# Moving the buffers of streamed operands off their common 2048-byte phase in SBUF

## The chip, the cores and the metric

The kernel runs on one core of a Trainium2 chip. The metric is the device time of one execution in microseconds; where several runs are shown, the median counts. A core has TensorE (PE: matmuls, and loads of the block of weights that stays resident in the array), VectorE (DVE), ScalarE (ACT), GpSimd (POOL) and SyncE (SP, which issues the DMAs here). Operands lie in SBUF, 128 partitions side by side; an address below is a byte offset within each partition. Results of matmuls go to PSUM.

## The reference

Two layers over 1024 tokens of width 1024, in float32. Layer 0 mixes tokens by attention over a sliding window of 128, with a sink and partial rotary embedding; layer 1 by a gated linear recurrence (HGRN2). Each is followed by an MLP of width 4096.

```python
for layer in range(DEPTH):
    h = rmsnorm(x, mix_norm[layer])
    y = sliding_window_attention(h, ...) if layer % 2 == 0 else hgrn2_recurrence(h, ...)
    x = x + y
    h = rmsnorm(x, mlp_norm[layer])
    x = x + jnp.square(jax.nn.relu(h @ w_up[layer])) @ w_down[layer]
return rmsnorm(x, final_norm)
```

## The kernel before, in words

**Tiles.** Everything large is cut into tiles of 128 partitions by 512 floats (TH), which is 2048 bytes in each partition. The tokens are handled in two halves (NH) of 512. Each tile belongs to a tag, and BUFS (line 41) says how many buffers a tag has: 60 of "a", 18 of "t", 7 of "m", 5 each of "wr", "wh" and "wl". "p" and "q" are four PSUM tiles each. "a" holds what lives long: the residual stream x, the operands that PE streams against many weight blocks, sums of the down projection. "t" holds what lives briefly, "wr" raw weights as they come from memory, "m" sums of weights and the scores of the attention.

**A product.** A float32 product is made of three passes in a faster format: split (line 429) and weight_split (line 412) cut a value into a high part, which is a cast, and a low part, which is the difference to it. mm3 (line 394) then multiplies high by high, high weights by low operand, low weights by high operand, all into one PSUM tile. In the large products the resident block is 128 columns of "wh" or "wl" and the streamed operand is an "a" tile, whole (512 columns) or half (256); in the projection of the attention (qkv, line 1069) it is the other way round, with a block of "a" resident and the weights streamed. The rows of the profile name the streamed operand first: "p<-a,wh" streams "a" against a block of "wh". The products of the MLPs and of the recurrence's input are arranged by Strassen's scheme, so weights are added and subtracted on DVE ("m<-wr,wr") before they are split.

**The recurrence** (line 1353) forms its scores in six levels. In level lg each chunk of 64 columns is cut into blocks of H = 2^lg, and PE streams every second block (line 1361), which begins H floats into the chunk.

**Order.** Each operation is put down with its engine, cost, inputs and outputs, and a planner (order, line 185) plays the program through with these costs. It decides the order on every engine, which of two engines does a cast, and the slot of every buffer: when a buffer's last user is done, its slot goes back on a heap, and the next buffer of that tag takes the slot that came free first. The planner knows slots by their number, not by their address.

**Addresses.** issue (line 275) calls lay_out (line 473) before it emits the instructions. lay_out reserves SBUF in the order in which it asks: first eight small constants (lines 475 and 476), then each buffer of a, t, wr, wh and wl as one tile of 2048 bytes (lines 477 to 479). The small tiles ahead of them add up so that the first of these buffers begins on a multiple of 2048, and since each is 2048 bytes long, all 93 do. Tags that lay_out does not name (m, and constants made later) lie behind. An "m" buffer is as long as its largest tile, 128 by 4 by 130 floats, 2080 bytes. When an operation is emitted, View.place (line 76) asks Buf.handle (line 111) for the tile of its buffer, which takes the slot's place by the tag "a_17" and the like, and applies the slices of the view to it. All instructions are recorded under line 336.

**DMAs.** All go through SP's queue in the planner's order (dma, line 346): weights into wr, x into a and t, spilled tiles from a and t to memory ("d") and back, and at the end a to the output.

Of the kernel before, what the change touches and what calls it, by code (L numbers as in the profile page):

```python
# [2 lines left out]

# [7 lines left out]
F32 = mybir.dt.float32  # L11
# [6 lines left out]
P = 128  # L18
# [4 lines left out]
TH = T // NH  # L23
# [17 lines left out]
BUFS = {"a": 60, "t": 18, "m": 7, "sm": 8, "wr": 5, "wh": 5, "wl": 5, "p": 4, "q": 4}  # L41
CH = 64
LEVELS = 6
HOMES = "aaaaaaaaaaaa"
K_SPANS = ((-1, 3), (2, 6), (5, 8))


class View:
# [34 lines left out]
class Buf:  # L83
# [27 lines left out]
    def handle(self):  # L111
        if self.tile is None:
            tag = f"{self.tag}_{self.slot}"
            self.tile = self.pool.tile(self.shape, self.dtype, tag=tag, name=self.name, bufs=1)
        return self.tile


# [24 lines left out]
class Schedule:  # L142
# [132 lines left out]
    def issue(self, lay_out):  # L275
        ops = self.order()
        lay_out()
        for op in ops:
            op.ways[op.engine][0]()


class Net:
# [190 lines left out]
    def lay_out(self):  # L473

        for v in (self.par, self.ones, self.ident, self.prev_mask, self.mean, self.eps, self.neg, *self.square[:1]):
            v.buf.handle()
        for tag in ("a", "t", "wr", "wh", "wl"):
            for k in range(BUFS[tag]):
                self.pool.tile([P, TH], F32, tag=f"{tag}_{k}", name=f"{tag}_first{k}", bufs=1)

    def spread(self, y, n=TH, r=None):

# [553 lines left out]
    def k_tiles(self, i):  # L1036
        if self.ks[i] is None:
# [3 lines left out]
            for g, z in enumerate(self.kl[i]):  # L1041
                _, o = self.rows(g)
                self.memset(z[o].bitcast(F32).only("o"), 0.0, "Pool", late)
            if K_SPANS[i][0] < 0:
                for z in self.ks[i] + self.kl[i]:
# [51 lines left out]
    def keys_values(self, n, ps, r):  # L1097
# [14 lines left out]
        for gp in range(2):  # L1112
            self.transpose(pk[:, gp], k[:, gp * P : gp * P + P])
        for i, (first, end) in enumerate(K_SPANS):
            if not first <= n < end:
# [50 lines left out]
    def attend_block(self, g, n, stacks):  # L1166
        i = (n >= 3) + (n >= 6)
        c = slice((n - 1 - K_SPANS[i][0]) * P, (n + 1 - K_SPANS[i][0]) * P)
        tok = slice((n % BPH) * P, (n % BPH) * P + P)
# [485 lines left out]
```

## Time and profile before

| | us |
|---|---|
| median of 3 runs | 2102.72 |
| the three runs | 2101.64 to 2105.72 |
| the profiled execution | 2103.77 |
| its span, first to last instruction | 2102.0 |

A row of the costliest groups gives the line, engine and operation, output and inputs by tag, the shapes, the count, then busy microseconds and mean nanoseconds of one, then the idle time of the engine ahead of it and what ended that. "(+1 forms)" says that the group mixes shapes. A row of the timeline gives the start in microseconds from the span's start, the duration, and how many instructions were merged. A row of the chain gives start, duration and what held the chain. A row of waits gives who waited for whom, the sum, the number of times and the longest. A row of one tile gives minimum, median and maximum duration in nanoseconds. A row of the DMA issues gives the number, the size and the median time to landing.

### The profile page before, as it was taken

Reading aid. Unit: us, or ns where it says so; the run is one execution under the profiler, and the core shown is the slowest. Engines: PE = TensorE matmul, PEld = TensorE weight load, DVE = VectorE, ACT = ScalarE, POOL = GpSimd, SP = SyncE. Lnnn points to the kernel's source line nnn. Section 1 sums busy time; section 2 is a strip of 40 time slices with the busy share of each in tenths; the row PEclk is TensorE's granted clock in tenths of the full one; section 3 lists DMA queues with packets and bytes.
Section 4 is the critical chain, followed back from the end, with each engine's and each line's share of the span. In section 5 each row is a group of like instructions: output and inputs, shape, how many; then the busy total and the mean of one; then the engine's idle time right before and its main releaser. Section 6 shows DMA issues by size and latency. Waiting matters only on the chain.

```text
span 2102.0 us, 35648 instructions
## 1 busy us (share of the span) xinstructions
PE 2068.4 (98%) x12220; PEld 1738.6 (83%) x12220; DVE 1898.4 (90%) x3922; ACT 1120.0 (53%) x2284; POOL 61.0 (3%) x121
## 2 busy tenths in 40 slices
PE   9999999999999999999999999999999999999998
PEld 7778777888888887888888888888788888888887
DVE  8889899999999989999889888888999999998995
ACT  5567777656565323556444444443755656432453
POOL 4030000000000000000000000000000000000000
PEclk9999999999999999999999999999999999999999
DMA  6212277867778967732322232576787777896742
GB/s 214 79 51 81 86 239 245 297 224 248 231 240 289 313 220 245 236 136 76 101 98 99 96 101 97 202 234 221 270 267 229 244 228 250 284 321 211 238 133 80
DMA packets 225845, 407.43 MB, mean 194 GB/s; under 512 B 25344, under 2 KB 30464, under 8 KB 225664
## 3 DMA queue, kind: packets, MB, share of 16 engines
q1 hardware_dynamic: 225664, 405.16, 58.5%
q8 instruction: 96, 1.57, 0.3%
q14 instruction: 85, 0.70, 0.1%
HBM read 321.17 MB, written 83.89 MB: 193 GB/s over the span
## 4 chain that ended last, share of the span: by engine, by line
PE 38%; DVE 11%; DMA 4%; issue 3%; ACT 1%; POOL 0%; SPq 0%; POOLq 0%; DVEq 0%; ACTq 0%
PE p L336 22%; PE q L336 16%; DVE t L336 4%; DVE a L336 3%; DMA wr<-in_down 2%; DVE wl L336 2%; DVE m L336 2%; ACT t L336 1%; DMA t<-d 1%; DMA wr<-in_up 1%; DMA d<-t 0%; DVE wh L336 0%; DMA wr<-in_win 0%; DMA a<-d 0%; ACT wh L336 0%
## 5 line engine op out<-in xcount | busy, mean ns | idle before, releaser
L336 PE MATMUL p<-a,wh 128*128 128x512 f32 (+1 forms) x2880 | 809.9, 365 | 3.2 <-DVE a L336 2.4
L336 PE MATMUL q<-a,wh 128*128 128x512 f32 x2112 | 654.6, 391 | 7.4 <-ACT t L336 6.1
L336 PEld LDWEIGHTS p<-a,wh 128*128 128x128 f32 x2880 | 514.6, 189 | 89.1 <-DVE a L336 4.0
L336 PE MATMUL p<-a,wl 128*128 128x512 f32 (+1 forms) x1440 | 521.0, 362 | 0.4 <-DVE wl L336 0.4
L336 PEld LDWEIGHTS q<-a,wh 128*128 128x128 f32 x2112 | 389.1, 188 | 85.3 <-ACT t L336 8.4
L336 PE MATMUL q<-a,wl 128*128 128x512 f32 x1056 | 411.1, 390 | 1.7 <-DVE wl L336 1.7
L336 PEld LDWEIGHTS p<-a,wl 128*128 128x128 f32 x1440 | 271.6, 189 | 40.9 <-DVE wl L336 1.3
L336 DVE TENSOR_TENSOR wl<-wr,wh 128x512 fp32r<-128x512 f32 x352 | 240.8, 685 | 6.7 <-ACT wh L336 1.3
L336 DVE TENSOR_TENSOR wl<-m,wh 128x512 fp32r<-128x512 f32 x338 | 230.1, 686 | 10.6 <-ACT wh L336 1.4
L336 PEld LDWEIGHTS q<-a,wl 128*128 128x128 f32 x1056 | 198.3, 188 | 45.6 <-DVE wl L336 3.7
L336 ACT ACTIVATE t<-t 128x512 f32<-128x512 f32 x268 | 168.8, 632 | 122.3 <-DVE t L336 114.9
L336 ACT CAST wh<-wr 128x512 fp32r<-128x512 f32 x249 | 154.0, 619 | 142.8 <-PE p L336 94.7
L336 DVE TENSOR_TENSOR t<-t,t 128x512 f32<-128x512 f32 (+3 forms) x337 | 197.4, 599 | 17.0 <-DMA t<-d 9.9
L336 ACT CAST a<-t 128x512 fp32r<-128x512 f32 (+1 forms) x216 | 130.1, 611 | 148.5 <-PE q L336 78.7
L336 DVE TENSOR_TENSOR a<-t,a 128x512 fp32r<-128x512 f32 (+2 forms) x314 | 205.9, 677 | 2.2 <-ACT a L336 1.7
L336 ACT CAST wh<-m 128x512 fp32r<-128x512 f32 x231 | 143.1, 620 | 113.8 <-PE p L336 47.4
L336 ACT COPY t<-q 128x512 f32<-128x512 f32 (+2 forms) x201 | 112.2, 559 | 104.1 <-PE q L336 87.3
L336 DVE TENSOR_TENSOR m<-wr,wr 128x512 f32<-128x512 f32 (+1 forms) x188 | 120.9, 645 | 17.6 <-DMA wr<-in_down 13.0
L336 PE MATMUL p<-wh,a 128*128 128x512 f32 x384 | 124.9, 396 | 0.7 <-ACT a L336 0.7
L336 DVE TENSOR_TENSOR t<-t,p 128x256 f32<-128x256 f32 x294 | 118.0, 414 | 0.3
L336 PEld LDWEIGHTS q<-t,t 128*64 128x64 f32 (+1 forms) x2160 | 95.4, 144 | 13.6 <-issue 7.6
L336 PE MATMUL q<-t,t 128*64 128x32 f32 (+2 forms) x2160 | 105.3, 229 | 0.0
(129 smaller groups left out, 2392.7 us busy)
## 6 DMA issues: line engine op xcount, KB each, us to landing
t<-d SPq DMA_DIRECT2D x548, 256.0 KB, 4.1
d<-t SPq DMA_DIRECT2D x244, 256.0 KB, 2.7
wr<-in_down SPq DMA_DIRECT2D x224, 256.0 KB, 4.2
wr<-in_up SPq DMA_DIRECT2D x178, 256.0 KB, 3.9
wr<-in_win SPq DMA_DIRECT2D x68, 256.0 KB, 2.9
a<-d SPq DMA_DIRECT2D x60, 256.0 KB, 4.7
wr<-in_wqkv SPq DMA_DIRECT2D x48, 256.0 KB, 2.9
d<-a SPq DMA_DIRECT2D x48, 256.0 KB, 3.9
```

What stands on the lines that cost most here:

```text
L336: fn(*[place(a) for a in args], **{k: place(v) for k, v in kw.items()})
```

## The change

Every second buffer of "a", those with an odd number, is reserved 16 bytes (four floats) longer, and its data begins behind these 16 bytes. lay_out asks for the "a" buffers last, behind t, wr, wh and wl, so that those four tags still begin on multiples of 2048.

```diff
+SKIP = {f"a_{k}": 4 for k in range(1, BUFS["a"], 2)}
...
     def handle(self):
         if self.tile is None:
             tag = f"{self.tag}_{self.slot}"
-            self.tile = self.pool.tile(self.shape, self.dtype, tag=tag, name=self.name, bufs=1)
+            skip = SKIP.get(tag, 0)
+            if skip:
+                n = math.prod(self.shape[1:])
+                whole = self.pool.tile([self.shape[0], skip + n], self.dtype, tag=tag, name=self.name, bufs=1)
+                self.tile = whole[:, skip:]
+                if len(self.shape) == 3:
+                    self.tile = self.tile.rearrange("p (a b) -> p a b", a=self.shape[1])
+            else:
+                self.tile = self.pool.tile(self.shape, self.dtype, tag=tag, name=self.name, bufs=1)
         return self.tile
...
-        for tag in ("a", "t", "wr", "wh", "wl"):
+        for tag in ("t", "wr", "wh", "wl", "a"):
             for k in range(BUFS[tag]):
-                self.pool.tile([P, TH], F32, tag=f"{tag}_{k}", name=f"{tag}_first{k}", bufs=1)
+                name = f"{tag}_{k}"
+                self.pool.tile([P, TH + SKIP.get(name, 0)], F32, tag=name, name=f"{tag}_first{k}", bufs=1)
```

More of the change, by code (lines that the diff above doesn't have):

```diff
@@ L1 @@
 import heapq
+import math
 from contextlib import ExitStack
```

## The prediction

> **What bounds the kernel.** I read the page first: busy shares, granted clock, the costliest groups, the chain.
>
> ```profile
> span 2102.0 us, 35648 instructions
> ...
> PE 2068.4 (98%) x12220; PEld 1738.6 (83%) x12220; DVE 1898.4 (90%) x3922; ACT 1120.0 (53%) x2284; POOL 61.0 (3%) x121
> ...
> PEclk9999999999999999999999999999999999999999
> ...
> PE 38%; DVE 11%; DMA 4%; issue 3%; ACT 1%; POOL 0%; SPq 0%; POOLq 0%; DVEq 0%; ACTq 0%
> ...
> L336 PE MATMUL p<-a,wh 128*128 128x512 f32 (+1 forms) x2880 | 809.9, 365 | 3.2 <-DVE a L336 2.4
> L336 PE MATMUL q<-a,wh 128*128 128x512 f32 x2112 | 654.6, 391 | 7.4 <-ACT t L336 6.1
> ...
> L336 PE MATMUL p<-a,wl 128*128 128x512 f32 (+1 forms) x1440 | 521.0, 362 | 0.4 <-DVE wl L336 0.4
> ...
> L336 PE MATMUL q<-a,wl 128*128 128x512 f32 x1056 | 411.1, 390 | 1.7 <-DVE wl L336 1.7
> ```
>
> TensorE (PE) is busy for 98% of the span, its clock is full in every slice, and its four largest groups are the ones the change touches: in "p<-a,wh" the streamed operand is an "a" buffer, the resident weight block a "wh" buffer. Together these groups hold 2880 + 2112 + 1440 + 1056 = 7,488 matmuls. The chain covers only 57% of the span, but in what it covers PE has two thirds.
>
> Next, what PE waits for. The view of waits on PE has twelve rows; the first and the last are
>
> ```profile
> PE q L336 <- ACT t L336: 8.9, 11, 2.5
> ...
> PE p L336 <- DVE wl L336: 0.4, 1, 0.4
> ```
>
> and the twelve add up to 26.7 us, 1.3% of the span. So the kernel runs at the pace of PE's own stream, and the question is whether the address of a streamed operand sets that pace. Matmuls overlap, so their durations (365 to 391 ns) do not give the pace; the starts in the timeline do. A stretch with 512 columns and one with 256:
>
> ```profile
> 702.19 0.61 PE L336 MATMUL q<-a,wh 128*128 128x512 f32 x2
> 702.64 0.39 PE L336 MATMUL q<-a,wl 128*128 128x512 f32 x1
> ...
> 704.91 0.61 PE L336 MATMUL p<-a,wh 128*128 128x512 f32 x2
> ```
> ```profile
> 473.08 0.40 PE L336 MATMUL p<-a,wh 128*128 128x256 f32 x2
> 473.32 0.28 PE L336 MATMUL p<-a,wl 128*128 128x256 f32 x1
> ...
> 474.88 0.40 PE L336 MATMUL p<-t,wh 128*128 128x256 f32 x2
> ```
>
> Twelve matmuls start between 702.19 and 704.91: 2.72 / 12 = 226.7 ns each. Fifteen start between 473.08 and 474.88: 120.0 ns each. The 256 columns between the two sizes cost 106.7 ns, 0.417 ns a column; what is left, 120.0 - 106.7 = 13.3 ns, is a fixed gap of 32 column times in each matmul. That gap is the only part of the stream that could be a collision. Over the matmuls with an "a" buffer streamed (the 7,488, and 264 + 128 more of "p<-a,a" and "q<-a,a" below, 7,880 in all) it is 7,880 x 13.3 ns = 105 us.
>
> ```profile
> L336 PEld LDWEIGHTS p<-a,a x264: 187/192/192, 754.7 to 2090.5; 128*128 128x128 f32 x132
> ...
> L336 PEld LDWEIGHTS q<-a,a x128: 186/188/192, 82.8 to 276.0; 128*128 128x128 f32 x128
> ```
>
> **The change part by part.** No instruction is added, removed or reordered: the planner's costs and buffer numbers know nothing of addresses, and the tiles that lay_out reserves issue nothing. The five queues, SP's with its DMAs too, hold what they held. What changes is where things lie. The first tiles go t, wr, wh, wl, a, so the weights stay on multiples of 2048 bytes, and each odd "a" buffer leaves out 16 bytes ahead of its data. An "a" buffer then starts up to some hundred bytes past a multiple of 2048, so weights and streamed operand no longer begin at the same phase. What is allocated later (the m tiles, small constants) moves up. So the costs are those of reading and writing at other addresses, engine by engine.
>
> *PE, streamed operand.* No large matmul of before streams from such an address. The nearest rows are the small ones of the recurrence. Its levels stream columns that begin 2^level floats into their chunk: the second group of 64 instructions (levels 1 and 2) begins 8 and 16 bytes past the boundary, the third (levels 3 and 4) 32 and 64 bytes.
>
> ```profile
> 983.83 1.99 PE q L336 x64
> ...
> 993.29 1.99 PE q L336 x64
> ...
> 1003.67 1.99 PE q L336 x64
> ```
>
> Both take 1.99 us: a start of 16 bytes costs less than the 0.01 us the view resolves, under 0.2 ns an instruction. These matmuls have 32 columns and two share the array, so the row bounds without proving. For the range I let the long ones gain or lose four column times (the 16 bytes skipped are four columns): 7,880 x 4 x 0.417 ns = 13.1 us, either way; the whole gap, 105 us, is the far end below. I take 0, by the levels' rows and because the pace is the same 0.417 ns a column at both sizes.
>
> *PE, weight loads.* Where "a" is the resident block ("p<-wh,a"), a load at an odd address has a row: the transposes of the m tiles, whose rows are 130 floats, 520 bytes, apart, so that three in four start 8, 16 or 24 bytes past a multiple of 32.
>
> ```profile
> L336 PE MATMUL q<-c,t 128*128 128x128 f32 x136 | 22.0, 277 | 3.4 <-DVE t L336 1.9 <-ACT t L336 1.5
> ...
> L336 PE MATMUL q<-c,m 128*128 128x128 f32 x128 | 19.5, 275 | 0.5 <-DVE m L336 0.2
> ```
>
> 275 ns against 277 ns from aligned t: cost 0.
>
> *DVE and ACT.* The m tiles again give the row: 2080 bytes each, so they lie on no common multiple of 2048, while wr does.
>
> ```profile
> L336 DVE TENSOR_TENSOR wl<-wr,wh 128x512 fp32r<-128x512 f32 x352 | 240.8, 685 | 6.7 <-ACT wh L336 1.3 <-PE q L336 0.5 <-DVE wh L336 0.5
> L336 DVE TENSOR_TENSOR wl<-m,wh 128x512 fp32r<-128x512 f32 x338 | 230.1, 686 | 10.6 <-ACT wh L336 1.4
> ...
> L336 ACT CAST wh<-wr 128x512 fp32r<-128x512 f32 x249 | 154.0, 619 | 142.8 <-PE p L336 94.7 <-PE q L336 27.2 <-DMA wr<-in_down 5.5
> ...
> L336 ACT CAST wh<-m 128x512 fp32r<-128x512 f32 x231 | 143.1, 620 | 113.8 <-PE p L336 47.4 <-PE q L336 41.4 <-DVE m L336 24.8
> ...
> L336 DVE CAST wh<-m 128x512 fp32r<-128x512 f32 x107 | 45.6, 426 | 33.6 <-PE p L336 16.7 <-PE q L336 16.6
> ...
> L336 DVE CAST wh<-wr 128x512 fp32r<-128x512 f32 x103 | 43.5, 422 | 26.0 <-PE p L336 20.4 <-DMA wr<-in_wqkv 2.9 <-PE q L336 2.4
> ...
> L336 DVE CAST a<-t 128x512 fp32r<-128x512 f32 x18 | 7.6, 422 | 2.9 <-ACT t L336 1.6 <-DMA t<-d 1.2
> ```
>
> One to four ns either way; I take 0. The worst would be that a cast on DVE loses its quick form (422 against 685 ns): with "a" written there are 18 + 18 of them, with "a" read 24, so 60 x 263 ns = 15.8 us on an engine that is idle for 2102.0 - 1898.4 = 203.6 us. PE hides it; at DVE's 11% of the chain it would show as 1.7 us.
>
> *DMAs.* Rows of 2 KiB now begin inside a larger block.
>
> ```profile
> a<-d SPq DMA_DIRECT2D x60, 256.0 KB, 4.7
> ...
> d<-a SPq DMA_DIRECT2D x48, 256.0 KB, 3.9
> ...
> a<-in_x SPq DMA_DIRECT2D x16, 256.0 KB, 5.3
> ...
> out<-a SPq DMA_DIRECT2D x16, 256.0 KB, 2.1
> d<-a SPq DMA_DIRECT2D x24, 128.0 KB, 2.8
> ```
>
> No DMA of before shows such a start. From below the cost is nothing, since nothing is moved that was not. From above, a row that is cut in two costs what two half rows do: 2 x 2.8 - 3.9 = 1.7 us a transfer. Few are waited for. On the chain stands one into "a":
>
> ```profile
> 1942.21 4.94 DMA a<-d
> ```
>
> With four odd buffers among the first eight loads of x, and the last store, that is 1.7 x (1 + 4 + 1) = 10.2 us at most. I take 0: the row stays whole and 2 KiB long, nearest to the 3.9 us.
>
> [...]
>
> **The sum.** 0 on PE, DVE, ACT and DMA. The profiled execution took 2103.77 us, 1.8 us around its span of 2102.0; the median of the runs shown is 2102.72, 1.05 lower. So: 2103 us.
>
> **The rivals.**
>
> *A: faster, the gap was a collision.* Weights and streamed operand begin at the same phase in before; if the load of the next block (128 floats, 512 bytes, 32 pieces of 16 bytes) takes one column time from the stream for each piece, that would make exactly 32. For it: the number fits. Against it: weight blocks begin at 0, 512, 1024 and 1536 bytes, streamed halves at 0 or 1024, t and "a" alike, and the gap is 13.3 ns in both stretches; the loads of the two rows above last 186 to 192 ns throughout. Price: from -13 us (four column times: 2090) to -105 us (all: 1998). [...]
>
> *B: slower, a start inside a larger block costs a read more.* Place: every matmul that streams from "a"; price: four column times, +13 us, 2116; it decides from 4.2 us / 7,880 = 0.53 ns a matmul. For it: no long stream from such an address is in the trace, and PE has no slack. Against it: the 1.99 us of the levels.
>
> *C: slower by the DMAs.* +10 us, 2113, by the bound above; it needs the worst price at each place that waits.
>
> *The change does not do what it says*: if rounding of lengths put the buffers back on equal phases, the time would stay; this lies in the forecast.
>
> **How the numbers follow.** A measurement of this kernel can tell about 0.2%, 4.2 us, from no change (its three runs lie 4.1 us apart), so "same" is 2099 to 2107. No change has 0.49: every row at an odd address is level with its aligned twin, but none of them is a long stream. A has 0.22, of it 0.10 below 2088, since the 13.3 ns are there to be won in every matmul. B has 0.19, some 0.06 beyond 2120, where it costs more than four column times. C has 0.10. Faster is A; slower is B and C, 0.29. The range runs from A's near price with 2 us to spare, 2088, to B's with 4, 2120; outside lie 0.10 + 0.06 = 0.16.
>
> **What would show it.** Right: starts 226.7 and 120.0 ns apart as before, the four groups at 365, 391, 362 and 390 ns, wl<-m at 686 ns, "a<-d" landing in 4.7 us. A shows as a shorter pace at the same 0.417 ns a column; B as a longer one with only "a" streamed, while "p<-t,wh" stays at 120.0; C as longer landings of d<-a and a<-d with an unchanged pace, and longer waits of DVE for them. Wrong I am above all if a long stream behaves unlike one of 32 columns.

## The result, and the profile after

The changed kernel takes 2116.48 us (three runs, 2114.90 to 2118.24) against 2102.72: a ratio of 1.0062, 95% interval 1.0042 to 1.0081, so 13.8 us slower by the medians. The forecast of no change is wrong. The time lies inside the stated range of 2088 to 2120, where rival B had put it, but not for B's reason, as the experiments show.

The page of the changed kernel, the same parts as before:

```profile
span 2114.7 us, 35648 instructions
...
PE 2090.2 (99%) x12220; PEld 1737.4 (82%) x12220; DVE 1901.4 (90%) x3922; ACT 1121.6 (53%) x2284; POOL 60.6 (3%) x121
...
PEclk9999999999999999999999999999999999999999
...
L346 PE MATMUL q<-a,wh 128*128 128x512 f32 x2112 | 662.4, 395 | 2.5 <-ACT t L346 1.9
...
L346 PE MATMUL q<-a,wl 128*128 128x512 f32 x1056 | 415.4, 394 | 1.1 <-DVE wl L346 1.1
```

The instructions are the same in number, the clock is full as before (0.998 granted in both), DVE and ACT are busy for as long as before within 3 us. Only PE has more to do: 2090.2 us against 2068.4, and it now fills 99% of the span. A 512-column matmul lasts 4 ns longer (395 against 391, 394 against 390). That is inside the stream, not ahead of it: the idle time in front of the first group fell from 7.4 to 2.5 us.

The groups kept apart by shape show that the two sizes moved in opposite directions. After:

```profile
L346 PE MATMUL p<-a,wh 128*128 128x512 f32 x2096 | 672.2, 399 | 0.2 <-ACT t L346 0.2
...
L346 PE MATMUL p<-a,wh 128*128 128x256 f32 x784 | 143.8, 281 | 0.2 <-DVE t L346 0.2
...
L346 PE MATMUL p<-wh,a 128*128 128x512 f32 x384 | 126.1, 399 | 1.4 <-ACT a L346 1.4
```

and the same groups before:

```profile
L336 PE MATMUL p<-a,wh 128*128 128x512 f32 x2096 | 664.4, 395 | 2.9 <-DVE a L336 2.4 <-ACT t L336 0.5
...
L336 PE MATMUL p<-a,wh 128*128 128x256 f32 x784 | 145.5, 283 | 0.3 <-DVE t L336 0.3
...
L336 PE MATMUL p<-wh,a 128*128 128x512 f32 x384 | 124.9, 396 | 0.7 <-ACT a L336 0.7
```

512 columns: 395 to 399 ns. 256 columns: 283 to 281 ns, shorter. And "p<-wh,a", where the streamed operand is a weight buffer that still begins on a multiple of 2048 and only the resident block has another phase, went from 396 to 399 ns as well. A streamed read that costs a little more wherever it starts off its block fits neither of the last two.

The timeline of PE in the changed kernel gives the pace:

```profile
702.12 0.62 PE L346 MATMUL p<-a,wh 128*128 128x512 f32 x2
702.58 0.39 PE L346 MATMUL p<-a,wl 128*128 128x512 f32 x1
...
704.89 0.63 PE L346 MATMUL q<-a,wh 128*128 128x512 f32 x2
```

Twelve matmuls start between 702.12 and 704.89, 230.8 ns each; before it was 226.7. Over the whole trace, from the starts of all matmuls, leaving out distances over 245 ns (waits, and changes of kind): the 6,888 of 512 columns start 227.8 ns apart before and 231.9 after, 28.2 us more; the 1,764 of 256 columns with wh or wl 119.7 and 118.4 ns, 2.2 us less. What lies in those longer distances shrank by 13.4 us. The sum, about 12.6 us, is close to the growth of the span, 12.7 us (2114.7 - 2102.0). So a slower stream of 28 us shows as 13, because PE stood still for less time between its streams. One row of PE's waits shows where some of it went, after:

```profile
PE q L346 <- ACT t L346: 4.7, 9, 1.3
```

It was 8.9 us. All PE waits together are 17.6 us after and 26.7 before, so they name 9.1 of the 13.4 us; the rest lies in long distances that the view of waits does not name.

The even pace itself is gone: in before 5,249 of 6,674 such distances of 512 columns are 226 or 227 ns, in the changed kernel 472 of 6,682.

The other steps of the prediction, in the rows after:

```profile
a<-d SPq DMA_DIRECT2D x60, 256.0 KB, 4.4
...
d<-a SPq DMA_DIRECT2D x48, 256.0 KB, 3.9
...
a<-in_x SPq DMA_DIRECT2D x16, 256.0 KB, 5.4
...
out<-a SPq DMA_DIRECT2D x16, 256.0 KB, 2.2
...
d<-a SPq DMA_DIRECT2D x24, 128.0 KB, 2.7
```
```profile
L346 DVE TENSOR_TENSOR a<-t,a 128x512 fp32r<-128x512 f32 x226 | 151.8, 682 | 0.7 <-ACT a L346 0.2
...
L346 DVE CAST a<-t 128x512 fp32r<-128x512 f32 x18 | 7.6, 421 | 2.3 <-ACT t L346 1.4 <-DMA t<-d 0.9
```

The DMAs land in the same time within 0.3 us, some sooner. DVE is as quick at the new addresses (682 against 684 ns before, 421 against 422), and the casts of ACT into "a" take 619 ns as before.

### The profile page after: what moved, and what is told of

Read it like the earlier page. It is cut to its first block, busy times and chain, and to the rows that moved or that the text cites. A ratio compares the mean times of both kernels' runs of the same rounds, so it can differ in the third digit from the quotient of the medians.

```text
span 2114.7 us, 35648 instructions
## 1 busy us (share of the span) xinstructions
PE 2090.2 (99%) x12220; PEld 1737.4 (82%) x12220; DVE 1901.4 (90%) x3922; ACT 1121.6 (53%) x2284; POOL 60.6 (3%) x121
## 4 chain that ended last, share of the span: by engine, by line
PE 86%; DVE 8%; issue 2%; ACT 2%; DMA 1%; POOL 0%; POOLq 0%; SPq 0%; ACTq 0%; DVEq 0%
PE p L346 44%; PE q L346 41%; DVE t L346 4%; DVE a L346 2%; ACT t L346 1%; DVE m L346 1%; DVE wl L346 1%; ACT a L346 1%; DMA a<-in_x 0%; DMA t<-d 0%; DVE wh L346 0%; DMA c<-in_par 0%; DMA d<-t 0%; ACT wh L346 0%; ACT m L346 0%
## 5 line engine op out<-in xcount | busy, mean ns | idle before, releaser
L346 PE MATMUL q<-a,wh 128*128 128x512 f32 x2112 | 662.4, 395 | 2.5 <-ACT t L346 1.9
L346 PE MATMUL q<-a,wl 128*128 128x512 f32 x1056 | 415.4, 394 | 1.1 <-DVE wl L346 1.1
L346 PEld LDWEIGHTS q<-t,t 128*64 128x64 f32 (+1 forms) x2160 | 95.5, 144 | 13.8 <-issue 7.7
```

The source lines that it names most:

```text
L346: fn(*[place(a) for a in args], **{k: place(v) for k, v in kw.items()})
```

## The experiments

In the program, tiles are rounded up to 32 bytes, so an odd "a" buffer takes 2080 bytes, and each of the 60 buffers begins 16 bytes further along its 2048 than the one before it: 0, 16, 32 and on to 944. "Phase" below is a start modulo 2048. PE loads and multiplies at the same time: in the trace before, the load of the next block (188 or 189 ns) runs for at least half of its time beside an earlier matmul in 7,435 of the 7,488 loads of the four largest groups, and PEld is busy for 83% of the span, PE for 98%. Theories, put up after the comparison: **Start** (rival B: each stream that begins off its block pays), **Step** (neighbouring streams must share a phase, whatever it is), then **Relative** (what counts is the distance from streamed to resident operand, modulo 256 bytes). Other engines and the moved m tiles were rivals too.

**All but the phases: e1_order.** The order of the changed kernel, and 960 bytes behind "a", so that m and later constants stand where it has them.

```diff
-        for tag in ("a", "t", "wr", "wh", "wl"):
+        for tag in ("t", "wr", "wh", "wl", "a"):
             for k in range(BUFS[tag]):
                 self.pool.tile([P, TH], F32, tag=f"{tag}_{k}", name=f"{tag}_first{k}", bufs=1)
+        self.pool.tile([P, 240], F32, tag="gap", name="gap", bufs=1)
```

> The a buffers lie last, as in the changed kernel, with 960 bytes behind them, so that the m tiles and later constants stand where the changed kernel has them; but every a buffer begins on a multiple of 2048. If the phases of the a buffers are the cause (theories Step and Start), the time is that of before, 2103 us (2099 to 2107), with 512-column matmuls 227 ns apart. If the new order or the moved m tiles are the cause, it is that of after, 2116.

Measured: 2103.02 us, ratio 1.0002 (0.9987 to 1.0016). The row of its 512-column stream:

```profile
L336 PE MATMUL q<-a,wh 128*128 128x512 f32 x2112 | 655.5, 392 | 4.2 <-ACT t L336 3.3 <-ACT wh L336 0.7
```

So neither the order nor the moved tiles cost anything that this interval could tell, and what remains for the 13.8 us is the phases of "a". On which engine they act this run does not say, since no "a" buffer has another phase in it.

**One phase for all: e2_uniform.** Against e1_order, no gap behind "a" but one of 32 bytes ahead of it.

```diff
+            if tag == "a":
+                self.pool.tile([P, 8], F32, tag="gap", name="gap", bufs=1)
```

> All 60 a buffers begin 32 bytes past a multiple of 2048, all at the same phase. Theory Step (PE's stream falls into a step with its weight loads and keeps it as long as every stream begins at the same phase): 2103 us, starts 227 ns apart as before. Theory Start (each stream that begins inside a larger block costs some columns, rival B of the prediction): 2116 us, starts 232 ns apart.

Measured: 2123.59 us, ratio 1.0106 (1.0085 to 1.0128), slower than the changed kernel.

```profile
L336 PE MATMUL q<-a,wh 128*128 128x512 f32 x2112 | 664.9, 396 | 2.4 <-ACT t L336 2.3
...
L336 PE MATMUL p<-a,wh 128*128 128x256 f32 x784 | 143.0, 280 | 0.0
```

512 columns 396 ns, starts 233.2 ns apart; 256 columns 280 ns, shorter than before. Theory Step, which I held then, falls: all streams share a phase, and the even pace is gone all the same. Start has the direction and nearly the pace (232), but not the time (2116), and it has no reason for the shorter 256 columns.

**Two phases: e3_two.** In the order of e1_order, even "a" buffers on multiples of 2048, odd ones 32 bytes past.

```diff
-        for tag in ("a", "t", "wr", "wh", "wl"):
-            for k in range(BUFS[tag]):
+        for tag in ("t", "wr", "wh", "wl", "a"):
+            for k in sorted(range(BUFS[tag]), key=lambda k: (tag == "a" and k % 2, k)):
+                if (tag, k) == ("a", 1):
+                    self.pool.tile([P, 8], F32, tag="gap", name="gap", bufs=1)
```

> Even a buffers on multiples of 2048, odd ones all 32 bytes past one: two phases instead of sixty. Theory Step: a change of phase between most neighbouring streams (high and low part), so slower than before, 2108 to 2116 us, 512-column starts 229 to 232 ns apart on average. Theory Start: half of the streams pay, 2109 us, and those from even buffers stay at 227 ns.

Measured: 2116.02 us, ratio 1.0072 (1.0054 to 1.0089).

```profile
L336 PE MATMUL q<-a,wh 128*128 128x512 f32 x2112 | 662.2, 395 | 3.0 <-ACT t L336 2.9
```

By the phase of the streamed "a" buffer (the planner's slots set beside the trace), the starts are 232.7 ns apart where it is 32 and 230.0 where it is 0. Start had wanted 227 for the latter. An aligned stream pays as well: 229.0 between two aligned ones, 230.4 between two that are off. The time and the average pace (231.4) are at the upper edge of what Step had said, but e2_uniform had already refuted it.

**PE alone: e5_alone.** Nothing but matmuls, in groups of 48 with chosen addresses; the streamed tile cycles through four places 2048 bytes apart, the resident block through 0, 512, 1024 and 1536. Four matmuls of 320 columns at other addresses stand between two groups, so each group starts from a disturbed pace. The core of it:

```python
for i in range(MANY):
    m, r = 512 * (i % 4) + moving[i] // 4, resident[i] // 4
    nc.tensor.matmul(ps[:, :n], ws[:, r : r + P], xs[:, m : m + n], start=i == 0, stop=i == MANY - 1)
```

> Only PE at work: streams of 48 matmuls at chosen addresses of streamed operand and weights, nothing else running; all of the reference's computation is left out. Theory Step: with all streams at one phase (zero, even) 226.7 ns apart whatever the phase; with phases that alternate, advance or are mixed (flip, step, mixed) 229 to 236 ns; 256 columns 120 ns at one phase and near 118 mixed. Theory Start: even as slow as flip and mixed, 231 to 233 ns. Theory Others (PE is held up by other engines' accesses at the new addresses): every group at 226.7 ns, since no other engine runs.

The groups, named by their PSUM tile (evenb: all streams 32 bytes on; evene: 256; flipf: every second 512 on; mixed: phases mixed; wmixed: those of the weights mixed):

```profile
L70 PE MATMUL evenb<-xs,ws 128*128 128x512 f32 x48 | 11.4, 395 | 0.0
...
L70 PE MATMUL mixed<-xs,ws 128*128 128x512 f32 x48 | 11.3, 394 | 0.0
...
L70 PE MATMUL wmixed<-xs,ws 128*128 128x512 f32 x48 | 11.3, 394 | 0.0
...
L70 PE MATMUL evene<-xs,ws 128*128 128x512 f32 x48 | 11.1, 389 | 0.0
L70 PE MATMUL zero<-xs,ws 128*128 128x512 f32 x48 | 11.0, 389 | 0.0
...
L70 PE MATMUL flipf<-xs,ws 128*128 128x512 f32 x48 | 11.0, 389 | 0.0
```

From the starts of the last 40 of each group, in ns: zero, flipf 226.7; evene 226.7 (after some irregular starts); evena (16) 231.8, evenb (32) 233.3, evenc (64) 228.9, evend (128) 232.2; flipa to flipd 230.0 to 232.5; mixed 232.0, wmixed 231.6; weights alone moved by 16 bytes 233.3. So the effect is PE's own: no other engine runs, which ends theory Others. Step falls again, since evena to evend keep one phase; Start fits three of these four, but not evenc. Shifting the weights alone does much the same as shifting the streams, which Start in rival B's form does not allow, and 256 bytes are as good as 0. The loads themselves do not get longer: 188 ns on average in zero, 189 with the weights moved by 16 bytes, 188 in wmixed.

**Both moved: e6_all.** A gap of 32 bytes ahead of t, wr, wh, wl and a together.

```diff
+        self.pool.tile([P, 8], F32, tag="gap", name="gap", bufs=1)
-        for tag in ("a", "t", "wr", "wh", "wl"):
+        for tag in ("t", "wr", "wh", "wl", "a"):
```

> Streamed operands and weights alike (t, wr, wh, wl, a) begin 32 bytes past a multiple of 2048. Theory Relative (what counts is the distance of a streamed start from a resident start, modulo 256 bytes): 2103 us, 512-column starts 227 ns apart. Theory Absolute (each of PE's reads has to begin on a multiple of 256 bytes for the even pace): 2116 to 2124 us, starts 231 to 233 ns apart.

Measured: 2104.23 us, ratio 1.0012 (1.0003 to 1.0022).

```profile
L336 PE MATMUL q<-a,wh 128*128 128x512 f32 x2112 | 654.4, 391 | 3.6 <-ACT t L336 2.9 <-ACT wh L336 0.6
```

The 512-column duration is back at 391 ns and the starts at 227.8. "a" is as far off its 2048 as in e2_uniform, which took 2123.59 us. What remains, 0.1%, is at the edge of what can be told. Start falls here, and with it Absolute, the form of it in which each of the two operands pays by itself for being off its block.

**Only the weights moved: e4_weights.** A gap of 32 bytes ahead of each buffer of wh and wl; "a" stays.

```diff
+                if tag in ("wh", "wl"):
+                    self.pool.tile([P, 8], F32, tag=f"gap_{tag}{k}", name=f"gap_{tag}{k}", bufs=1)
```

> The a buffers stay on multiples of 2048; the ten buffers of wh and wl begin at ten other phases, 32 to 320 bytes past one, of which one is a multiple of 256. Theories Relative and Absolute: slower, 2112 to 2122 us, 512-column starts 230 to 233 ns apart. Theory Streamed (only where the streamed operand begins matters): 2103 us, 227 ns.

Measured: 2118.42 us, ratio 1.0083 (1.0068 to 1.0099), with every "a" buffer where it was before. The 512-column starts are 232.1 ns apart, so theory Streamed falls.

```profile
L336 PE MATMUL q<-a,wh 128*128 128x512 f32 x2112 | 662.0, 394 | 1.3 <-ACT t L336 1.0
```

**A whole period: e8_far.** As e2_uniform, but with 256 bytes in the gap.

```diff
-                self.pool.tile([P, 8], F32, tag="gap", name="gap", bufs=1)
+                self.pool.tile([P, 64], F32, tag="gap", name="gap", bufs=1)
```

> All a buffers begin 256 bytes past a multiple of 2048. If the pattern repeats every 256 bytes, as the streams with PE alone say: 2103 us, 512-column starts 227 ns apart. If in the whole kernel a longer distance counts, as slow as the shift by 32 bytes: 2124 us, 233 ns.

Measured: 2100.87 us, ratio 1.0002 (0.9990 to 1.0014), 512-column starts 227.8 ns apart.

```profile
L336 PE MATMUL q<-a,wh 128*128 128x512 f32 x2112 | 656.2, 392 | 2.3 <-ACT wh L336 1.0 <-ACT t L336 1.0
```

So in the whole kernel too the pattern repeats after 256 bytes.

**The scan: e7_scan.** PE alone again, with other addresses.

```diff
+    shift = lambda d: [b + d for b in blocks]
...
+    for name, d in (("botha", 16), ("bothb", 32), ("bothc", 64), ("bothd", 128)):
+        yield name, 512, [d] * MANY, shift(d)
...
+    deltas = [4, 8] + list(range(16, 256, 16))
+    for k, d in enumerate(deltas):
+        yield "full" + chr(97 + k), 512, [d] * MANY, blocks
+    for k, d in enumerate(deltas):
+        yield "half" + chr(97 + k), 256, [d] * MANY, blocks
```

> PE alone, 48 matmuls in each group; all of the reference's computation is left out. Relative: botha to bothd (streamed and resident shifted alike) 226.7 ns; pairnext (each streamed start at the phase of the block that loads beside it) near 227, pairown as slow as mixed, 232; full groups (streamed shifted by 4, 8, 16 and on in steps of 16 to 240 bytes) 229 to 235, lowest near 0 and 256. Absolute: both groups 231 to 235, pairnext and pairown like mixed. 256 columns: 120.0 at shift 0, 116 to 119 elsewhere under either.

Starts, ns apart: streamed and resident both moved by 32, 64 or 128 bytes 226.7 to 226.8, as Relative says. Both by 16 bytes, though, 233.3: at distance 0 as well these 16 bytes cost 6.6 ns, which Relative had not; which of the two operands pays is not told apart. Streamed by 32: 233.3, the weights by 224, the same distance modulo 256: 233.4. Streamed by 224: 233.4, the weights by 32: 233.4. These four fit the distance but would fit it with either sign. All other distances cost something at 512 columns, from 228.9 (64) to 236.9 (4); that the cost is lowest close to 0 and 256 was expected and is wrong, since 4 and 240 bytes are the worst.

My guess at which pair counts missed: with mixed phases, pairing each stream with its own block (231.8) or with the one that loads beside it (232.6) helps no more than mixed does (232.3). So distance 0 from each stream to one block is not enough; shown is the even pace where all streams share one phase, all blocks share one, and the two agree modulo 256. Nor do the addresses settle everything: streams 128 bytes on, the same addresses, took 232.2 ns in e5_alone and 233.2 here, each in a rhythm of its own.

At 256 columns two distances stand out:

```profile
L66 PE MATMUL halfzero<-xs,ws 128*128 128x256 f32 x48 | 5.9, 283 | 0.0
...
L66 PE MATMUL halfi<-xs,ws 128*128 128x256 f32 x48 | 5.6, 276 | 0.0
L66 PE MATMUL halfn<-xs,ws 128*128 128x256 f32 x48 | 5.6, 276 | 0.0
```

At distance 0 they start 120.0 ns apart, at 112 (halfi) 113.5 and at 192 (halfn) 113.3; elsewhere 116.6 to 119.9, and 123.3 at 4 bytes.

**Put to use: e9_brief.** The "t" buffers are streamed only by the short matmuls (256 columns and less). In the order of e1_order, a gap of 48 floats ahead of t and of 16 behind it puts t alone 192 bytes off a multiple of 256.

```diff
-        for tag in ("a", "t", "wr", "wh", "wl"):
+        for tag in ("t", "wr", "wh", "wl", "a"):
+            gap = {"t": 48, "wr": 16}.get(tag)
+            if gap:
+                self.pool.tile([P, gap], F32, tag=f"gap_{tag}", name=f"gap_{tag}", bufs=1)
```

> Only the t buffers move: they begin 192 bytes past a multiple of 256, all else on multiples of 256. Streams of 256 columns from t against wh and wl (588 of them) should then start 113.3 ns apart, as with PE alone at that distance, in place of 120.0, and all others as before: 588 x 6.7 ns = 3.9 us less, 2099 us. Rival: the small streams of the recurrence and the accesses of DVE and ACT to t mind the new start, and the time is 2103 us or more.

Measured: 2098.97 us, ratio 0.9987 (0.9977 to 0.9997), faster than both kernels by a little.

```profile
L336 PE MATMUL p<-t,wh 128*128 128x256 f32 x392 | 71.1, 279 | 0.0
```

It was 283 ns. The starts are 116.4 ns apart (119.7 before), not 113.3. With PE alone it took four matmuls at 192 bytes until the short pace was reached, and here 256-column streams from "a", at distance 0, come between; that this keeps the pace from settling is likely and not shown. By the rows, 588 x 3.5 ns = 2.1 us of the 3.9 hoped for, which agrees with the ratio (0.13%, 2.7 us). That the time meets the 2099 expected is in part luck: the runs of before beside it had a median of 2100.97 and not 2103.

## Where the prediction held and where it failed, step by step

**What bounds the kernel** held: PE's own stream sets the time (PE is busy for 98% of the span before and 99% after), and a longer pace, 231.9 ns in place of 227.8, is what made the changed kernel slower. **DMA, DVE and ACT at 0** held, by the rows above at the new addresses. Rival C is out: the landings did not grow.

The step that failed first is "PE, streamed operand": "I take 0, by the levels' rows and because the pace is the same 0.417 ns a column at both sizes." Both reasons were weak. The levels are short: 32 columns, two in the array at once (in the trace before, the two of a pair start 6 or 7 ns apart and last 223 ns each on average); the sentence that said so was right, and the row should have carried no weight. What the prediction named as its main sign of being wrong, a long stream that behaves unlike one of 32 columns, is what came: the 6,888 matmuls of 512 columns start 4.1 ns further apart, 28 us of stream where the sum had 0. The second reason took two points for a line. The gap of 32 column times at 512 and at 256 columns is no constant: with PE alone at distance 0 it is 32 at 320, 384 and 496 columns (146.7, 173.3 and 220.0 ns) but 28 at 288 (131.6), 38 at 448 (202.7) and 40 at 480 (216.8); at 256 it falls to 16 at distance 112 or 192 (113.5 and 113.3 ns), and at 512 it is 45 with mixed phases. So the gap of before belonged to its addresses. Why it has these sizes at these lengths, no run shows.

"PE, weight loads" at 0 failed as well. It stood on the durations of short transposes (275 against 277 ns), and the change moves the resident block in "p<-wh,a", whose starts went from 228.9 to 232.3 ns apart. In e4_weights the weights alone cost 0.83%, and with PE alone and the streams left in place the pace went from 226.7 to 233.3 ns when the weights alone moved by 16 bytes. The loads do not last longer (188 or 189 ns on average before and after in the four largest groups); it is the streams beside them that follow each other more slowly.

Rival A was nearest in kind: the pace depends on where weights and streamed operand lie to each other. For 512 columns it had the sign reversed, since the equal phases are the good case (226.7 ns with PE alone, against 228.9 to 236.9 at the other distances tried). For 256 columns it was right that part of the gap can be won, 6.7 ns of the 13.3 with PE alone.

The trace of before held a warning that I did not use. In it, 512-column matmuls that follow 256-column ones start irregularly for some five matmuls (here 233, 236, 228, 233 and 230 ns apart) and only then keep 227:

```profile
475.60 0.63 PE L336 MATMUL q<-a,wh 128*128 128x512 f32 x2
476.07 0.39 PE L336 MATMUL q<-a,wl 128*128 128x512 f32 x1
476.30 0.63 PE L336 MATMUL q<-a,wh 128*128 128x512 f32 x2
476.76 0.39 PE L336 MATMUL q<-a,wl 128*128 128x512 f32 x1
476.99 0.62 PE L336 MATMUL q<-a,wh 128*128 128x512 f32 x2
477.44 0.39 PE L336 MATMUL q<-a,wl 128*128 128x512 f32 x1
477.67 0.62 PE L336 MATMUL q<-a,wh 128*128 128x512 f32 x2
```

Pairs of 0.63 us in place of 0.61, the first three taking 0.70 us (475.60 to 476.30) and the third three 0.68 (476.99 to 477.67): a pace that has to be found can be lost. After the change it is not found again: no more than six starts in a row lie 225 to 228 ns apart, where before had runs of up to 426.

**Rival B's time** (2116) is right to the microsecond and its mechanism is not. Its 13.1 us were 7,880 x 1.7 ns; the runs show 4.1 ns on the 6,888 of 512 columns, a gain on those of 256, and half of the loss taken back from waits and other pauses of PE. The same sum with other terms is luck.

What stays open: why the distance counts. For 512 columns it is shown that distance 0 modulo 256 bytes gives 226.7 to 226.8 ns with both operands 0, 32, 64 or 128 bytes on, and 233.3 ns with both 16 bytes on; what inside PE or SBUF makes it so, no run shows.

## What to carry to other kernels

Where PE's stream is the bound, each matmul loads its own block and the streams are 512 columns long as here, let all streamed operands and all weights begin at the same phase modulo 256 bytes, on multiples of 32 (with PE alone, both 16 bytes on cost 6.6 ns a matmul); moving either alone off it cost 0.6 to 1.1% here, moving both by 32 bytes 0.1%. Another length can have other good distances, as 256 columns have at 112 and 192 bytes (113.5 and 113.3 ns). A pace that keeps to 225 to 228 ns over 426 starts in a row need not be a constant (after the change no more than six did): before calling a change of addresses free, look at the pace where it is disturbed. And where the engine that bounds the kernel still has pauses, a loss in its stream shows only in part (28 us of stream, 13 us of time), so read the groups and not the total.

## What the runs showed of the hardware that was not expected

With PE alone, 48 matmuls of 512 columns start 226.7 ns apart when streamed and resident operands are at distance 0 modulo 256 bytes, and 228.9 to 236.9 at the other distances tried. 256 columns have their best distances elsewhere, 113.3 to 113.5 ns at 112 and 192 bytes against 120.0 at 0. With both operands 16 bytes off they start 233.3 ns apart, with both 32 off 226.7 to 226.8. Single runs of the kernel before went from 2095.0 to 2108.2 us, a spread of 0.6%. So the 0.1% of e9_brief and of e6_all lies at the edge of what the intervals can tell, and e9_brief's gain rests on its rows, while the shifts of "a" or of the weights alone, e8_far apart, stand clear of no change by their intervals and by their rows.
